# Gathered expert rows two units ahead, one pool for the weight rows, split dot products and another order of the gathers

## The chip, the core and the metric

The kernel runs on one core of a Trainium2 chip. The time is the device time of one execution in microseconds (us), the median of three runs. The core has five engines that run their own instruction lists in order and wait for each other by semaphores: TensorE (PE: matmuls; PEld is its weight load), VectorE (DVE), ScalarE (ACT), GpSimd (POOL) and SyncE (SP), which here only issues transfers. Indirect transfers (gathers) are issued on POOL. 16 DMA engines move the data.

## The reference

One decoder layer over 512 tokens of width 2048: RWKV-7 time mixing beside Mamba-2, an output projection, then an expert layer (PEER). The change lies in the expert layer alone. For each token it picks, in 8 heads, 16 of 16384 experts:

```python
q = (xb @ w_query).reshape(PEER_BLOCK, PEER_HEADS, 2, PEER_HALF)
s = jnp.einsum('lhpd,hpnd->lhpn', q, sub_keys).astype(jnp.float32)
s_half, i_half = lax.top_k(s, PEER_TOPK)
...
top_s, pos = lax.top_k(cand_s, PEER_TOPK)
eidx = jnp.take_along_axis(cand_i, pos, axis=-1)
gates = jax.nn.softmax(top_s, axis=-1)
u = u_emb[eidx]
act = jax.nn.gelu(jnp.einsum('ld,lhkd->lhk', xb, u), approximate=False)
return jnp.einsum('lhk,lhkd->ld', gates * act, v_emb[eidx])
```

`u_emb` and `v_emb` are 16384 x 2048 float32 tables, 134 MB each. A residual add and a final RMSNorm follow.

## The kernel before

The first 1640 us (projections, scan, output projection, queries and top-k) are the same code before and after, but for the pool that the query weights pass through. Then the 512 tokens are treated in two ways.

**320 tokens (TD) go dense, through all experts.** `expert_u(i)` multiplies 128 experts' u with the tokens: four quarter rows of 256 KB are loaded (`load_split`), each is split into a high part (a ScalarE cast, line 193) and a low part (a POOL subtraction, line 194), and TensorE does 3 matmuls for each of 16 blocks, 48 in all (lines 197 to 199). 128 such calls cover u. `expert_v(grp)` does the same with v for 512 experts in four quarters; a quarter again has four splits (`vhi`, `vlo`) and 48 matmuls, into `po`, which VectorE adds to `hT` (line 1197). One `expert_u` or one quarter of `expert_v` is called a unit; there are 256. Between the two, `gate_block` builds the gate matrix with two VectorE operations per token (J and I2, lines 1115 and 1116) and a matmul, by way of DRAM (`glD`); `expert_g` multiplies gates and activations on VectorE (line 1155) and splits them (`glo`). The first 30 `expert_u` stand ahead of the first `expert_v`; their activations go through DRAM.

**192 tokens (TG) are gathered.** Each slot gathers 128 rows of 8 KB, 1 MB, by an indirect transfer that POOL issues (line 1225). A u slot is a row per token, and one VectorE instruction multiplies it with the token's row and sums it (the dot, line 1230). 128 tokens have 128 slots (`("u", 0, n)`); the other 64 lie twice on the partitions and have 64 (`("u", 1, n)`). A v slot is the 128 rows of one token, and TensorE sums them with weights: four slots are collected, then four parts (`part(q)`) of 16 small matmuls go out (line 1245, `pw`). A part is written to DRAM (`yG`); `gathered()` reads it back, adds and normalises.

**What sets the order.** `pace(ins)` is called after each unit. It uses the rows gathered at the last call, then issues at most two gathers, as long as fewer than NGB rows are held and the slots lie behind units / NGU. A part is taken from `parts` after each split in `expert_v`. The instruction order on each engine is then made by a scheduler from this trace of calls. Rows for u and v have their own pools: `wr` 3 quarter rows with 3 pairs of high and low parts (pool `wp`), `vr` 3 half rows (512 KB) with 3 pairs (pool `vp`).

Of the kernel before, what the change touches and what calls it, by code (L numbers as in the profile page):

```python
# [10 lines left out]
F32 = mybir.dt.float32  # L11
# [8 lines left out]
P = 128  # L20
T = 512
# [5 lines left out]
TD = 320  # L27
NGU = 236
TG = T - TD
TB = 32  # L30
NGB = 6
NACT = 9
NSP = 30
# [96 lines left out]
def _hybrid(st, tc, nc, I, out):  # L130
# [56 lines left out]

    copied = []
    done_mm = [None]

# [43 lines left out]
    with ExitStack() as sb:  # L234
# [97 lines left out]

        wp = sc.enter_context(tc.tile_pool(name="wp", bufs=3, reuse_waits="tile"))
        bp = sb.enter_context(tc.tile_pool(name="bp", bufs=1, reuse_waits="tile"))
        lora = bp.tile([P, 3, T], F32, name="lora")
# [6 lines left out]
        def load_split(w, q, n):  # L342

            wr = wp.tile([P, n, P], F32, name="wr", bufs=3)
            nc.sync.dma_start(wr, w[:, q:q + n, :])
            whi = wp.tile([P, n, P], F32R, name="whi")
            wlo = wp.tile([P, n, P], F32R, name="wlo")
            return whi, wlo, split(whi, wlo, wr, G)

        def project_to(pss, ws, xhi, xlo, ahead=()):  # L350

            nk = ws.shape[2]
            ahead = list(ahead)
            for q in range(0, nk, 4):
                n = min(4, nk - q)
                for j, ps in enumerate(pss):
                    whi, wlo, last = ahead.pop(0) if ahead else load_split(ws[j], q, n)
                    for i in range(n):
                        k = q + i
                        mm3(ps, whi[:, i, :], wlo[:, i, :], xhi[k], xlo[k], k == 0, k == nk - 1)  # L360
            return last

# [573 lines left out]


    pu = st.enter_context(tc.tile_pool(name="pu", bufs=2, space=PSUM, reuse_waits="tile"))
    pw2 = st.enter_context(tc.tile_pool(name="pw2", bufs=1, space=PSUM, reuse_waits="tile"))
# [4 lines left out]
    gt_st = ExitStack()  # L944
    va = st.enter_context(tc.tile_pool(name="va", bufs=NACT, reuse_waits="tile"))
    gq = st.enter_context(tc.tile_pool(name="gq", bufs=1, reuse_waits="tile"))
# [4 lines left out]

    n2t = gq.tile([P, D], F32, name="row")
    n2D = dp.tile([P, D], F32, name="n2D")
    yG = dp.tile([TG, D], F32, name="yG")
# [4 lines left out]
    with ExitStack() as s3:  # L959
# [17 lines left out]
        for k in range(KT):  # L977
            t = qp.tile([P, T], F32, name="t")
            for h, c in ((hT[k], slice(0, TD)), (hG[k], slice(TD, T))):
                V.scalar_tensor_tensor(t[:, c], h, w2[:, k:k + 1], rr[:, c], OP.mult, OP.mult)  # L980
            nc.sync.dma_start(hGD[:, k, :], hG[k])
            nf = qp.tile([P, T], F32, name="nf")
            if k % 2:
                V.tensor_scalar_add(nf, t, mod2[:, 16 + k:17 + k])
            else:
                S.activation(nf, t, AF.Identity, bias=mod2[:, 16 + k:17 + k])
            split(nhi[k], nlo[k], nf[:, 0:TD], V if k % 4 == 0 else G)
            split(ngh[k], ngl[k], nf[:, TD:T], V if k % 4 == 2 else G)
            if k % 4 == 0:
                pt = [pq.tile([P, 4, P], F32, name="sc") for _ in range(2)]  # L990
            TE.transpose(pt[0][:, k % 4, :], nf[:, T - P:T], ident)
            TE.transpose(pt[1][0:64, k % 4, :], nf[:, TD:TD + 64], ident)
            if k % 4 == 3:
                S.copy(n2t[:, P * (k - 3):P * (k + 1)], pt[0].rearrange("p a b -> p (a b)"))
                n2s = qp.tile([64, T], F32, name="n2s")
                S.copy(n2s, pt[1][0:64].rearrange("p a b -> p (a b)"))
                for half in range(2):
                    nc.sync.dma_start(n2D[64 * half:64 * half + 64, P * (k - 3):P * (k + 1)], n2s)
        skT = qp.tile([P, 16, P], F32, name="skT", bufs=1)
# [98 lines left out]

    hg_st.close()
    gr = st.enter_context(tc.tile_pool(name="gr", bufs=NGB, side="right", reuse_waits="tile"))  # L1100
    gx = gt_st.enter_context(tc.tile_pool(name="gx", bufs=2, reuse_waits="tile"))
# [4 lines left out]
    def gate_block(tb):  # L1106

        gb = gx.tile([P, P, TB], F32, name="gb", bufs=1)
        for q in range(TB // 4):
            ps = pg.tile([P, 4, P], F32, name="pg")  # L1110
            for i in range(4):
                t = TB * tb + 4 * q + i
                J = gx.tile([P, P], F32, name="J", bufs=12)
                I2 = gx.tile([P, P], F32, name="I2", bufs=12)
                V.tensor_scalar(J, iota, jT[:, t:t + 1], None, OP.is_equal)  # L1115
                V.tensor_scalar(I2, iota, iT[:, t:t + 1], gT[:, t:t + 1], OP.is_equal, OP.mult)  # L1116
                TE.matmul(ps[:, i], lhsT=J, rhs=I2, start=True, stop=True)
# [16 lines left out]

    slots = [("u", 0, n) for n in range(P)]
    for n in range(P):
        slots += [("u", 1, n // 2)] * (n % 2 == 0) + [("v", 64 + n)]
    slots += [("v", n) for n in range(64)]
    nslots = len(slots)
# [22 lines left out]
    def pace(ins):  # L1162

        nonlocal units
        units += 1
        with tc.issue_after(ins.ins):
            ready, begun[:] = begun[:], []
            for s in ready:
                use(*s)
            while slots and (nslots - len(slots)) * NGU < units * nslots and len(begun) < 2 and held[0] < NGB:  # L1170
                begun.append(gather(slots.pop(0)))

    vrows = I["v"].rearrange("(g i j) c -> g j i c", i=4, j=P)

    def expert_v(grp):
        nonlocal nu
        gh = ghl.pop(grp)
        for q in range(4):
            po = [pv.tile([P, TD], F32, name="po") for _ in range(4)]
            for i in range(4):  # L1180
                if i % 2 == 0:
                    vr = vp.tile([P, 2, 512], F32, name="vr", bufs=3)
                    nc.sync.dma_start(vr, vrows[grp][:, i:i + 2, 512 * q:512 * q + 512])
                vhi = vp.tile([P, 512], F32R, name="vhi", bufs=3)
                vlo = vp.tile([P, 512], F32R, name="vlo", bufs=3)
                last = split(vhi, vlo, vr[:, i % 2, :], G)
                for d in range(4):
# [16 lines left out]
            if not (slots or begun or parts or done):  # L1204
                done.append(True)
                gathered()
            if nu < min(128, 4 * grp + 12):
                pace(expert_u(nu))
                nu += 1

    wts = [gq.tile([P, n], F32, name=f"wts{n}") for n in (P, 64)]
    begun = []
    parts = []
    four = []
    held = [0]
    n2s = [n2t]

    def gather(s):
        g = gr.tile([P, D], F32, name="g")
        if s[0] == "u" and s[1] and s[2] == 0:  # L1220
            n2s.append(gq.tile([P, D], F32, name="row"))
            nc.sync.dma_start(n2s[1], n2D)
        held[0] += 1
# [4 lines left out]
    def use(g, kind, i, n=None):  # L1228
        if kind == "u":
            V.scalar_tensor_tensor(g, g, 1.0, n2s[i], OP.mult, OP.mult, accum_out=wts[i][:, n:n + 1])  # L1230
            held[0] -= 1
# [23 lines left out]
    def weights(i):  # L1255

        w = wts[i]
        S.activation(w, w, AF.Gelu)
        V.tensor_tensor(w, w, ggt[i], OP.mult)
# [50 lines left out]
    for grp in range(32):  # L1310
        expert_g(grp)
        expert_v(grp)


    rr = rms_all(pu, "mm", gq, sacc[:, 0:TD])
# [29 lines left out]
```

## Time and profile before

| | |
|---|---|
| median of 3 runs | 4291.24 us (4290.52 to 4294.44) |
| the profiled execution | 4301.42 us |
| its span, first to last instruction | 4299.7 us |
| busy: PE / DVE / ACT / POOL | 90% / 56% / 33% / 58% of the span |
| mean granted TensorE clock | 0.930 of full speed |
| moved | 956.51 MB, mean 222 GB/s |
| dots on VectorE (line 1230) | 192, mean 3095 ns |
| subtractions on POOL, u and query / v | 832, mean 1366 ns / 512, mean 1420 ns |

A busy PE is not a PE at its peak: each dense matmul's record is 0.31 us long, while the next starts about 0.15 us after it. So TensorE's pace is read from starts, not from its busy share. The granted clock is 1.0 at 2.4 GHz and 0.5 at 1.2 GHz; values between are mixtures. Idle time of an engine that nobody waits for costs nothing.

### The profile page before, as it was taken

The page shows a single profiled execution, that of the slowest core. Times are in us where ns is not written, and L with a number is a line of the kernel's source. Part 1 is how long each engine was busy: PE and PEld are TensorE (multiplying, and loading weights), DVE is VectorE, ACT ScalarE, POOL GpSimd, SP SyncE. Part 2 cuts the span into 40 slices and gives each one's busy share as a digit, 9 for nine tenths or more (in the row PEclk, how much of TensorE's full clock was granted, in tenths as well). Part 3 has the DMA queues.
Part 4 walks back from the last instruction along what each step waited for, and adds up shares of the span by engine and source line. Part 5 has one row for each costly group of instructions (what it writes and reads, how often), then busy time and mean ns, then how long its engine had stood idle before and what let it go on. Part 6 is the DMA issues. An engine that isn't in the chain of part 4 may idle for free.

```text
span 4299.7 us, 64989 instructions
## 1 busy us (share of the span) xinstructions
PE 3870.1 (90%) x23694; PEld 3119.5 (73%) x23694; DVE 2414.9 (56%) x4523; ACT 1427.3 (33%) x2780; POOL 2507.4 (58%) x1919
## 2 busy tenths in 40 slices
PE   5899989999998997877788779999999999999976
PEld 3667657766667996776777768888787788777736
DVE  7442254556516999992778874445555545422204
ACT  3443233333324222332222223333333333333313
POOL 5455434423236334455777888777777778766633
PEclk9999989978979998888899889999999999999977
DMA  8456642242433226667877878888788888877762
GB/s 341 169 186 208 193 122 77 77 122 78 154 106 106 72 83 243 234 243 247 295 261 273 317 264 294 302 310 295 282 298 302 303 307 309 295 265 256 275 236 97
DMA packets 373681, 956.51 MB, mean 222 GB/s; under 512 B 57904, under 2 KB 123312, under 8 KB 317872
## 3 DMA queue, kind: packets, MB, share of 16 engines
q1 hardware_dynamic: 318064, 549.68, 38.7%
q0 software_dynamic: 55296, 402.68, 24.6%
q8 instruction: 186, 3.05, 0.3%
q14 instruction: 135, 1.11, 0.1%
HBM read 907.92 MB, written 44.24 MB: 221 GB/s over the span
## 4 chain that ended last, share of the span: by engine, by line
PE 63%; DVE 17%; DMA 8%; POOL 5%; issue 3%; ACT 1%; SPq 0%; POOLq 0%; DVEq 0%; ACTq 0%
PE mm L199 9%; PE mm L197 9%; PE mm L198 9%; PE pw L1245 7%; PE po L197 6%; PE po L199 6%; PE po L198 6%; DVE I L1116 3%; DVE g L1230 2%; DMA wr<-in_uT 2%; DVE J L1115 2%; POOL vlo L194 2%; POOL wlo L194 1%; DMA AI<-abD 1%; POOL g L1225 1%
## 5 line engine op out<-in xcount | busy, mean ns | idle before, releaser
L194 POOL TENSOR_TENSOR wlo<-wr,whi 128x512 fp32r<-128x512 f32 (+2 forms) x832 | 1127.6, 1366 | 965.9 <-ACT whi L193 866.5
L194 POOL TENSOR_TENSOR vlo<-vr,vhi 128x512 fp32r<-128x512 f32 x512 | 719.3, 1420 | 244.9 <-ACT vhi L193 211.6
L197 PE MATMUL mm<-n2hi,whi 128*128 128x320 f32 x2304 | 756.8, 329 | 53.7 <-ACT whi L193 52.9
L199 PE MATMUL mm<-n2hi,wlo 128*128 128x320 f32 x2304 | 751.9, 328 | 52.8 <-POOL wlo L194 52.6
L193 ACT CAST whi<-wr 128x512 fp32r<-128x512 f32 (+2 forms) x832 | 503.3, 616 | 861.9 <-PE mm L198 429.2
L198 PE MATMUL mm<-n2lo,whi 128*128 128x320 f32 x2304 | 741.6, 322 | 0.0
L197 PE MATMUL po<-ghi,vhi 128*128 128x320 f32 x2048 | 646.5, 322 | 50.6 <-DVE hT L1197 43.5
L1230 DVE SCALAR_TENSOR_TENSOR g<-g,row 128x2048 f32<-128x2048 f32 x192 | 591.6, 3095 | 168.7 <-DMA g<-in_u,eix 168.7
L198 PE MATMUL po<-glo,vhi 128*128 128x320 f32 x2048 | 640.4, 316 | 0.5 <-DVE glo L194 0.5
L199 PE MATMUL po<-ghi,vlo 128*128 128x320 f32 x2048 | 565.5, 320 | 51.2 <-POOL vlo L194 51.0
L193 ACT CAST vhi<-vr 128x512 fp32r<-128x512 f32 x512 | 312.9, 619 | 706.6 <-PE po L198 557.8
L199 PEld LDWEIGHTS mm<-n2hi,wlo 128*128 128x128 f32 x2304 | 456.6, 199 | 102.7 <-POOL wlo L194 68.2
L197 PEld LDWEIGHTS mm<-n2hi,whi 128*128 128x128 f32 x2304 | 458.0, 199 | 90.5 <-ACT whi L193 64.2
L197 PEld LDWEIGHTS po<-ghi,vhi 128*128 128x128 f32 x2048 | 394.9, 194 | 131.8 <-issue 57.9
L1197 DVE SCALAR_TENSOR_TENSOR hT<-po,mod,hT 128x320 f32<-128x320 f32 x512 | 250.8, 542 | 389.4 <-PE po L199 389.4
L198 PEld LDWEIGHTS mm<-n2lo,whi 128*128 128x128 f32 x2304 | 457.7, 199 | 14.1 <-issue 13.4
L199 PEld LDWEIGHTS po<-ghi,vlo 128*128 128x128 f32 x2048 | 370.4, 193 | 117.6 <-POOL vlo L194 68.8
L1155 DVE TENSOR_TENSOR act<-gd,act 128x320 f32<-128x320 f32 x128 | 214.1, 1687 | 422.4 <-ACT act L1128 392.2
L198 PEld LDWEIGHTS po<-glo,vhi 128*128 128x128 f32 x2048 | 396.3, 193 | 27.7 <-issue 26.8
L1245 PE MATMUL pw<-g,wT 128*32 128x512 f32 x1536 | 327.2, 631 | 31.2 <-DMA g<-in_v,eT 21.3
L1225 POOL DMA_INDIRECT g<-in_u,eix x192 | 247.8, 1291 | 93.7 <-PE pw L1245 23.8
L1225 POOL DMA_INDIRECT g<-in_v,eT x192 | 184.7, 962 | 160.9 <-DVE g L1230 75.5
(438 smaller groups left out, 5899.7 us busy)
## 6 DMA issues: line engine op xcount, KB each, us to landing
wr<-in_uT SPq DMA_DIRECT2D x512, 256.0 KB
vr<-in_v SPq DMA_DIRECT2D x256, 512.0 KB
wr<-in_wrest SPq DMA_DIRECT2D x160, 256.0 KB
aw<-in_ada SPq DMA_DIRECT2D x32, 1024.0 KB
a2w<-in_adar SPq DMA_DIRECT2D x64, 512.0 KB
glD<-gb SPq DMA_DIRECT2D x10, 2048.0 KB
gd<-glD SPq DMA_DIRECT2D x32, 640.0 KB
a3w<-in_adar SPq DMA_DIRECT2D x32, 512.0 KB
```

The costliest lines, as they stand in the source:

```text
L193: copied.append(S.copy(hi, src))
L194: return (eng or V).tensor_tensor(lo, src, hi.bitcast(F32), OP.subtract)
L197: TE.matmul(ps, lhsT=whi, rhs=xhi, start=first, stop=False)
L198: TE.matmul(ps, lhsT=whi, rhs=xlo, start=False, stop=False)
L199: done_mm[0] = TE.matmul(ps, lhsT=wlo, rhs=xhi, start=False, stop=last)
L1115: V.tensor_scalar(J, iota, jT[:, t:t + 1], None, OP.is_equal)
L1116: V.tensor_scalar(I2, iota, iT[:, t:t + 1], gT[:, t:t + 1], OP.is_equal, OP.mult)
L1155: V.tensor_tensor(a.rearrange("p (b t) -> p b t", t=TB), gd[:, :, i, :], a.rearrange("p (b t) -> p b t", t=TB), OP.mult)
L1197: V.scalar_tensor_tensor(h, po[d], mod2[:, 48 + k:49 + k], h, OP.mult, OP.add)
L1225: G.indirect_dma_start(out=g, out_offset=None, in_=I[s[0]], in_offset=bass.IndirectOffsetOnAxis(ap=ix, axis=0))
L1230: V.scalar_tensor_tensor(g, g, 1.0, n2s[i], OP.mult, OP.mult, accum_out=wts[i][:, n:n + 1])
L1245: TE.matmul(ps[32 * j:32 * j + 32, :], lhsT=wT[:, t0 + j:t0 + j + 1].to_broadcast([P, 32]), rhs=gs[j][:, cq], start=True, stop=True, tile_ ...
```

## The change

- **One pool.** When the output projection is done, pool `wp` is closed and another opened with ten quarter rows (`NRAW`) and four pairs of parts (`NSPL`); u and v rows share them. A v load is now a quarter row of 256 KB (512 loads instead of 256). J and I2 have 4 buffers instead of 12.
- **Gathers.** A gather's row is used two calls of `pace` later (`LEAD`). Seven rows instead of six, and the slots are laid over 200 units instead of 236. Parts are now also taken inside `project_to`, so in `expert_u` too. A loop at the end takes what is left.
- **Dots in halves.** A dot becomes two instructions of 1024 elements and one addition for all slots at the end.
- **Order of slots.** The 64 two-slot u gathers come first, then four v, then the 128 others with one v behind each second one, then the rest of v.
- The tokens' row (`row`) is loaded from DRAM for both groups, into one buffer. Activations have 6 buffers instead of 9, and `expert_u` runs at most 8 instead of 12 ahead.

```diff
-NGU = 236
+NGU = 200
-NGB = 6
-NACT = 9
+NGB = 7
+LEAD = 2
+NRAW = 10
+NSPL = 4
+NACT = 6
...
                         mm3(ps, whi[:, i, :], wlo[:, i, :], xhi[k], xlo[k], k == 0, k == nk - 1)
+                if parts:
+                    parts.pop(0)()
...
+    sc.close()
+    wp = st.enter_context(tc.tile_pool(name="wx", bufs=NSPL, reuse_waits="tile"))
+    nraw = NRAW
...
-                J = gx.tile([P, P], F32, name="J", bufs=12)
-                I2 = gx.tile([P, P], F32, name="I2", bufs=12)
+                J = gx.tile([P, P], F32, name="J", bufs=4)
+                I2 = gx.tile([P, P], F32, name="I2", bufs=4)
...
-    slots = [("u", 0, n) for n in range(P)]
+    slots = [("u", 1, n) for n in range(64)] + [("v", n) for n in range(4)]
     for n in range(P):
-        slots += [("u", 1, n // 2)] * (n % 2 == 0) + [("v", 64 + n)]
-    slots += [("v", n) for n in range(64)]
+        slots += [("u", 0, n)] + [("v", 4 + n // 2)] * (n % 2 and n < 120)
+    slots += [("v", n) for n in range(64, TG)]
...
-            ready, begun[:] = begun[:], []
-            for s in ready:
-                use(*s)
-            while slots and (nslots - len(slots)) * NGU < units * nslots and len(begun) < 2 and held[0] < NGB:
-                begun.append(gather(slots.pop(0)))
+            while begun and begun[0][0] <= units - LEAD:
+                use(*begun.pop(0)[1:])
+            for _ in range(2):
+                if slots and (nslots - len(slots)) * NGU < units * nslots and held[0] < NGB:
+                    begun.append((units,) + gather(slots.pop(0)))
...
-                if i % 2 == 0:
-                    vr = vp.tile([P, 2, 512], F32, name="vr", bufs=3)
-                    nc.sync.dma_start(vr, vrows[grp][:, i:i + 2, 512 * q:512 * q + 512])
-                vhi = vp.tile([P, 512], F32R, name="vhi", bufs=3)
-                vlo = vp.tile([P, 512], F32R, name="vlo", bufs=3)
-                last = split(vhi, vlo, vr[:, i % 2, :], G)
+                vr = wp.tile([P, 512], F32, name="vr", tag="wr", bufs=NRAW)
+                nc.sync.dma_start(vr, vrows[grp][:, i, 512 * q:512 * q + 512])
+                vhi = wp.tile([P, 512], F32R, name="vhi", tag="whi")
+                vlo = wp.tile([P, 512], F32R, name="vlo", tag="wlo")
+                last = split(vhi, vlo, vr, G)
...
-            if nu < min(128, 4 * grp + 12):
+            if nu < min(128, 4 * grp + 8):
...
-        if s[0] == "u" and s[1] and s[2] == 0:
-            n2s.append(gq.tile([P, D], F32, name="row"))
-            nc.sync.dma_start(n2s[1], n2D)
+        if s[0] == "u" and s[2] == 0:
+            n2s[s[1]] = va.tile([P, D], F32, name="row", bufs=1)
+            nc.sync.dma_start(n2s[s[1]], n2D[s[1]])
...
-            V.scalar_tensor_tensor(g, g, 1.0, n2s[i], OP.mult, OP.mult, accum_out=wts[i][:, n:n + 1])
+            for e in range(2):
+                c = slice(D // 2 * e, D // 2 * e + D // 2)
+                V.scalar_tensor_tensor(g[:, c], g[:, c], 1.0, n2s[i][:, c], OP.mult, OP.mult,
+                                       accum_out=wtp[i][:, e, n:n + 1])
...
+    while slots or begun or parts:
+        while parts:
+            parts.pop(0)()
+        pace(done_mm[0])
+    if not done:
+        gathered()
```

The instruction order of TensorE where the gates end (`pg` is a gate matmul, `mm` one of `expert_u`, `po` one of `expert_v`), before:

```order
L1117 MATMUL pg<-I_16623,J 128x128
L1117 MATMUL pg<-I_16628,J 128x128
L199 MATMUL mm<-n2hi_11444,wlo 128x320
L197 MATMUL mm<-n2hi_11445,whi 128x320
L198 MATMUL mm<-n2lo_11461,whi 128x320
```

and after:

```order
L1128 MATMUL pg<-I_16636,J 128x128
L1128 MATMUL pg<-I_16641,J 128x128
L201 MATMUL po<-ghi,vhi 128x320 x4
L202 MATMUL po<-glo,vhi 128x320
L203 MATMUL po<-ghi,vlo 128x320
```

Before, some ten units of `expert_u` follow the last gate; after, the last 50 gate matmuls stand together and `expert_v` follows at once.

POOL near unit 60, in the units of `expert_v` and `expert_u` that alternate (`g<-in_u` and `g<-in_v` are gathers), before:

```order
L1225 DMA g<-in_u,eix_11494 128x2048 x3
L194 TENSOR_TENSOR vlo<-vr,vhi 128x512 x3
L194 TENSOR_TENSOR wlo<-wr,whi 128x512 x2
L194 TENSOR_TENSOR vlo<-vr,vhi 128x512
L1225 DMA g<-in_u,eix_11494 128x2048 x3
```

and after:

```order
L198 TENSOR_TENSOR wlo<-wr,whi 128x512 x4
L198 TENSOR_TENSOR vlo<-vr,vhi 128x512
L1235 DMA g<-in_v,eT 128x2048
L1235 DMA g<-in_u,eix_11494 128x2048 x2
L1235 DMA g<-in_v,eT 128x2048
L198 TENSOR_TENSOR vlo<-vr,vhi 128x512
```

Gathers of v, which need no dot, have come between those of u.

TensorE at the last parts of the gathered tokens (`pw`; four matmuls are one part, and `mm<-ident,g` belongs to `gathered()`), before:

```order
L197 MATMUL po<-ghi,vhi 128x320
L198 MATMUL po<-glo,vhi 128x320
L1245 MATMUL pw<-g,wT 32x512 x4
L199 MATMUL po<-ghi,vlo 128x320 x4
L1245 MATMUL pw<-g,wT 32x512 x52
L1284 MATMUL mm<-ident,g 128x64
```

and after:

```order
L201 MATMUL po<-ghi,vhi 128x320
L202 MATMUL po<-glo,vhi 128x320
L203 MATMUL po<-ghi,vlo 128x320
L1258 MATMUL pw<-g,wT 32x512 x29
L1298 MATMUL mm<-ident,g 128x64
```

52 matmuls in a row have become 29. Behind them 384 dense matmuls (8 units) are left before, 1008 (21 units) after.

## Rows read from the trace of the kernel before

**Rows 1.** Line 194 by stretch: DVE (calls), POOL (calls), clock, DMA share, GB/s.

```profile
1640.00:2075.00 435.00, 1.69 (x4) 162.46 (x111) 0.86 0.71 255
2075.00:2600.00 525.00, 50.00 (x37) 296.45 (x202) 0.90 0.80 285
2600.00:3130.00 530.00, 43.47 (x28) 323.21 (x237) 0.99 0.83 296
3130.00:3750.00 620.00, 71.04 (x36) 370.90 (x272) 1.00 0.84 303
3750.00:4100.00 350.00, 26.32 (x19) 187.93 (x149) 1.00 0.74 268
4100.00:4300.00 200.00, 3.64 (x4) 49.22 (x39) 0.74 0.43 151
```

**Rows 2.** Timeline of PE from 3907: start, us, instruction.

```profile
3907.09 0.31 PE L198 MATMUL mm<-n2lo,whi 128*128 128x320 f32 x1
3907.32 1.06 PE L1245 MATMUL pw<-g,wT 128*32 128x512 f32 x8
3908.57 0.31 PE L197 MATMUL mm<-n2hi,whi 128*128 128x320 f32 x1
...
3911.80 0.31 PE L198 MATMUL mm<-n2lo,whi 128*128 128x320 f32 x1
```

**Rows 3.** Lines on DVE, 1640 to 1930: calls, busy us, mean ns, idle before.

```profile
L1116 DVE TENSOR_SCALAR I<-iota,iT,gT 128x128 f32<-128x128 f32 x314 | 145.0, 462 | 0.0
...
L1230 DVE SCALAR_TENSOR_TENSOR g<-g,row 128x2048 f32<-128x2048 f32 x33 | 80.7, 2475 | 0.0
```

**Rows 4.** Timeline of DVE and POOL from 2452.

```profile
2452.81 5.18 DVE L1230 SCALAR_TENSOR_TENSOR g<-g,row 128x2048 f32<-128x2048 f32 x1
...
2453.28 2.56 POOL L194 TENSOR_TENSOR vlo<-vr,vhi 128x512 fp32r<-128x512 f32 x2
...
2457.92 2.28 DVE L1230 SCALAR_TENSOR_TENSOR g<-g,row 128x2048 f32<-128x2048 f32 x1
2458.27 2.77 POOL L1225 DMA_INDIRECT g<-in_u,eix  x1 [2.44 <-DVE g L1230]
...
2460.14 2.28 DVE L1230 SCALAR_TENSOR_TENSOR g<-g,row 128x2048 f32<-128x2048 f32 x1
```

**Rows 5.** Lines, 2075 to 2600: dots and gather issues.

```profile
L1230 DVE SCALAR_TENSOR_TENSOR g<-g,row 128x2048 f32<-128x2048 f32 x79 | 263.2, 3351 | 19.7 <-DMA g<-in_u,eix 19.7
...
L1225 POOL DMA_INDIRECT g<-in_u,eix x79 | 123.1, 1558 | 26.8 <-issue 8.3 <-DVE g L1230 7.3 <-PE po L199 4.1
```

**Rows 6.** Line 1225, gathers: ns min/median/max, waits on POOL, landing.

```profile
L1225 POOL DMA_INDIRECT g<-in_v,eT x192: 933/940/1877, 2580.9 to 4170.0; - x192
...
  DVE g L1230: 89.4, 30
...
DMA to landing us min/median/max: 5.5/8.8/15.3
```

**Rows 7.** Chain of waits at the end: start, us, what.

```profile
4161.18 1.98 PE pw L1245 x8
...
4163.86 1.98 PE pw L1245 x8
...
4169.98 10.33 DMA g<-in_v,eT
...
4191.92 3.85 DMA yG<-ys
...
4217.03 1.00 PE mm L928 x4
...
4284.03 1.45 PE mm L928 x6
```

**Rows 8.** Waits from 1900 on: us in total, times, longest.

```profile
ACT whi L193 <- DMA wr<-in_uT: 152.4, 59, 8.0
```

**Rows 9.** Waits of PE, 3750 to 4100.

```profile
PE pw L1245 <- DMA g<-in_v,eT: 0.8, 1, 0.8
```

More of the change, by code (lines that the diff above doesn't have):

```diff
@@ L188, in _hybrid @@
     copied = []
+    parts = []
     done_mm = [None]
@@ L333, in _hybrid @@
         wp = sc.enter_context(tc.tile_pool(name="wp", bufs=3, reuse_waits="tile"))
+        nraw = 3
         bp = sb.enter_context(tc.tile_pool(name="bp", bufs=1, reuse_waits="tile"))
@@ L342, in load_split @@
         def load_split(w, q, n):
-            wr = wp.tile([P, n, P], F32, name="wr", bufs=3)
+            wr = wp.tile([P, n, P], F32, name="wr", bufs=nraw)
             nc.sync.dma_start(wr, w[:, q:q + n, :])
@@ L944, in _hybrid @@
     gt_st = ExitStack()
-    va = st.enter_context(tc.tile_pool(name="va", bufs=NACT, reuse_waits="tile"))
     gq = st.enter_context(tc.tile_pool(name="gq", bufs=1, reuse_waits="tile"))
@@ L950, in _hybrid @@
     gT = gp.tile([P, T], F32, name="gT")
-    n2t = gq.tile([P, D], F32, name="row")
-    n2D = dp.tile([P, D], F32, name="n2D")
+    n2D = dp.tile([2, P, D], F32, name="n2D")
     yG = dp.tile([TG, D], F32, name="yG")
@@ L993, in _hybrid @@
             if k % 4 == 3:
-                S.copy(n2t[:, P * (k - 3):P * (k + 1)], pt[0].rearrange("p a b -> p (a b)"))
-                n2s = qp.tile([64, T], F32, name="n2s")
-                S.copy(n2s, pt[1][0:64].rearrange("p a b -> p (a b)"))
+                n2s = qp.tile([P, T], F32, name="n2s")
+                S.copy(n2s, pt[0].rearrange("p a b -> p (a b)"))
+                nc.sync.dma_start(n2D[0][:, P * (k - 3):P * (k + 1)], n2s)
+                n2s = qp.tile([P, T], F32, name="n2s")
+                S.copy(n2s[0:64], pt[1][0:64].rearrange("p a b -> p (a b)"))
                 for half in range(2):
-                    nc.sync.dma_start(n2D[64 * half:64 * half + 64, P * (k - 3):P * (k + 1)], n2s)
+                    nc.sync.dma_start(n2D[1][64 * half:64 * half + 64, P * (k - 3):P * (k + 1)], n2s[0:64])
         skT = qp.tile([P, 16, P], F32, name="skT", bufs=1)
@@ L1099, in _hybrid @@
     hg_st.close()
+    va = st.enter_context(tc.tile_pool(name="va", bufs=NACT, side="right", reuse_waits="tile"))
     gr = st.enter_context(tc.tile_pool(name="gr", bufs=NGB, side="right", reuse_waits="tile"))
@@ L1211, in _hybrid @@
     wts = [gq.tile([P, n], F32, name=f"wts{n}") for n in (P, 64)]
+    wtp = [gq.tile([P, 2, n], F32, name=f"wtp{n}") for n in (P, 64)]
     begun = []
-    parts = []
     four = []
     held = [0]
-    n2s = [n2t]
+    n2s = {}
     def gather(s):
         g = gr.tile([P, D], F32, name="g")
-        if s[0] == "u" and s[1] and s[2] == 0:
-            n2s.append(gq.tile([P, D], F32, name="row"))
-            nc.sync.dma_start(n2s[1], n2D)
+        if s[0] == "u" and s[2] == 0:
+            n2s[s[1]] = va.tile([P, D], F32, name="row", bufs=1)
+            nc.sync.dma_start(n2s[s[1]], n2D[s[1]])
         held[0] += 1
@@ L1257, in weights @@
         w = wts[i]
+        V.tensor_tensor(w, wtp[i][:, 0], wtp[i][:, 1], OP.add)
         S.activation(w, w, AF.Gelu)
```

## The prediction

> **What bounds the kernel now.** I read the span in stretches first, then asked for each stretch which engine another one waits for. The unit of counting is a unit of dense work: one `expert_u` or one quarter of `expert_v`, each 4 splits and 48 matmuls, 256 in all. The split's subtraction on POOL (line 194) counts them: its calls by stretch, divided by 4, are units [rows 1]. About 3 units lie ahead of 1640 us; then 28 units take 435 us (15.5 each), 50.5 take 525 (10.4), 59 take 530 (8.95), 68 take 620 (9.1), 37 take 350 (9.4), and the last 10 take 200.
>
> TensorE's own price of a unit: dense matmuls start 0.147 us apart (22 starts from 3908.57 to 3911.80), so 48 are 7.04 us. Where one part of a gathered v (8 short matmul records) stands between them, two starts take 1.48 us (3907.09 to 3908.57) instead of 0.29, so a part costs 1.19 [rows 2]. There is one part per v row, 192 in all. From 3750 to 4100 two parts per unit give 7.04 + 2.38 = 9.4, which is what the stretch shows: TensorE is the bound there. Elsewhere it is not.
>
> In the 290 us up to 1930 VectorE has no idle time before its gate operations and dots [rows 3]. 33 dots at 2.28 leave 215 us for 314 gate pairs, 0.68 each. From 2075 to 2600 VectorE and POOL block each other. A dot that is 2.28 us alone lasts 5.18 when two subtractions (1.28 each) run inside it, and a gather issue that is 0.94 alone lasts 2.77 beside a dot [rows 4, 6]. A unit there has 4 subtractions (5.12), 1.56 dots (3.57) and 1.6 gather issues (1.5): 10.2 in sum, 10.4 measured [rows 1, 5]. So the sum of what POOL and VectorE do with SBUF operands is the price of a unit there, TensorE's 7 us notwithstanding, and the granted clock is 0.90. The last 200 us are a drain: the chain of waits alternates gathers of up to 10.3 us with v parts 2.68 us apart, at clock 0.74; then the gathered tokens' end runs from 4191.9 to 4217, and only then the last 8 units [rows 1, 7].
>
> **The change, part by part.** No computation goes; what moves is when things stand where. I counted gathers against units in the instruction order of both programs. Before: 49 gathers issued by unit 31, 219 by unit 141 (159 of them u), 384 by 256. After: 58, 235 (176 u), and 379 by unit 235.
>
> *Ahead of unit 31.* Gates now lie evenly between 30 units instead of 20, so V can't start before the last gate. VectorE needs 320 x 0.68 = 218 us of gates and 58 dots. A half dot was never run: at least 1.14 (half of 2.28), at most 1.14 plus a blocked subtraction, 2.4; I take 1.2, since a half saves nothing of its start, so 2.4 a dot, 139 us. Sum 357; J and I2 with four buffers instead of twelve and blocked dots make it 390 (my bounds 355 and 450), then some 25 us until the last gate block has gone through DRAM and V begins, in place of other units that used to cover it. That is 415 for what took 435: V begins near 2055 instead of 2075.
>
> *Units 31 to 141.* Dots go from 110 to 118 and gathers from 170 to 177, but before they crowd into the first 50 units. Evenly spread, a unit has 5.12 of subtractions, 1.07 dots at 2.4 (2.57) and 1.6 gather issues (1.5): 9.2, and TensorE's side is 7.04 plus half a part, 7.7. With the ratio of measured to summed (10.4 to 10.2) that is 9.4 a unit, 110 units in 1034 us instead of 1055. Bounds: 8.95, the price from 2600 to 3130 where a unit had half a dot, and 10.4, that of the crowded stretch.
>
> The loads' own part of this I cost at zero. ScalarE waited 152 us for u rows [rows 8], yet behind those waits stands the POOL sum, which does not shrink. Counted in the instruction order, ten shared quarter rows let a load go out 20 us and more of TensorE work ahead of its use (9 to 20 before). On the other hand four shared hi/lo pairs replace three and three; what queues behind a late split is the next gather, on POOL.
>
> *Units 141 to 235.* 94 units at 7.04 are 662; 128 v parts at 1.19 are 152; 2% for near ties, 16. Sum 830. Few dots are left here (16), so POOL's 5.12 + 1.5 stays below TensorE.
>
> *The end.* Before, 13 of the last v parts stand back to back behind all but 8 units. Now 7 do, with 21 units behind them. I charge 7 x 2.68 = 19, one gather wait of 10 and the same 25 for the gathered tokens: 54. Then 8 units at the 8.4 that the last 8 took (4217 to 4284 [rows 7]) and 13 at 7.04: 159. The close from 4284 on is unchanged, 16.
>
> Moved with these: the 128-token row is loaded from DRAM in one megabyte behind the 64th dot of the other group, on the sync queue ahead of later loads; at ten rows of stock that hides, and costs some 10 us if the stock is out. The 256 more load issues on that queue lie beside its waiting. The extra additions are two.
>
> **Sum**, against the profiled span of 4299.7: 2055 + 1034 + 830 + 54 + 159 + 16 = 4148, 152 less. The profiled execution took 4301.4 and the median is 4291.2; the same 152 off the median gives 4139, and I say 4140.
>
> **The rivals.**
> - *Loads and halves help more.* Waits of ScalarE on loads go, blocked POOL stretches halve, the crowded stretch reaches 8.7 a unit and the first one saves 40 more: 77 + 40 less, 4020. For it: those 152 us of waits. Against: no stretch with a dot has shown under 8.95.
> - *POOL and VectorE don't overlap at all.* The gather issue that began at 2458.27 waited out one dot and ended beside the next, which stayed at 2.28 us [rows 4], so some overlap exists. If a half dot locks POOL as a whole one did, and each hand-over costs a wait, a unit is 10.3: 110 x 0.9 = 99 more, 4240. The trace's 10.4 for a sum of 10.2 is close to no overlap already, which keeps it alive. The Trainium skill has this as a rule (SBUF — State Buffer, section "SBUF: two separate sides"): GpSimd and a VectorE operation with two SBUF inputs hold one port pair exclusively for the whole instruction. By that rule, halving a dot divides the longest block and leaves the sum; the 5.18 us dot agrees.
> - *The fourth gather of a token group is late.* After unit 141 a group's rows come free together, and the next group's last gather has 8 to 10 us of TensorE work to land, against 8.8 median [rows 6]. At 2.5 us for each of 32 groups: 80 more, 4220. Against it: the same distance held from 3750 to 4100, and TensorE's waits for gathers there are 0.8 us in sum [rows 9].
> - *Slower: gathers stand at POOL's head.* Seven rows with a lead of two units leave a gather waiting for the dot just queued. Each such wait was 3.0 us before (89.4 in 30) [rows 6], with the splits of the next unit behind it. If every unit from 31 to 141 pays one of them in half a unit's reach, 1.5 us, that is 165 more: 4305. It decides from 10.8 us a unit on. Against it: the lead also means that the dot no longer waits for its data (in the instruction order a v gather stands 3 units of TensorE work ahead of its use, 2.4 before).
>
> **Chances.** Forecast 0.52 (its own range 4095 to 4190), better 0.15, no overlap 0.12, late fourth gather 0.11, slower 0.10. This kernel's timing tells 0.2%, 8.6 us. From the slower case 0.07 lies above that and 0.03 within it; with some of the overlap case, faster 0.87, same 0.05, slower 0.08. Eight in ten: 4035, where the better case begins to be left out, to 4265.
>
> **What would show it.** Units by the subtraction's calls: 9.4 us from unit 31 to 141, 8.8 from there to 235, TensorE at clock 1.0; v parts before the last 160 us with no alternation of gathers and parts but one; VectorE's gates ending near 2030; ScalarE's waits for loads near zero. Wrong if a unit in the middle costs over 10, or POOL's waits for dots exceed 150 us.

## The result and the profile after

The changed kernel takes 4177.5 us (median of four runs, 4163.62 to 4187.0) where the kernel before takes 4292.56: a ratio of 0.9729, 95% interval 0.9699 to 0.976. Forecast was 4140, range 4035 to 4265. The profiled execution has a span of 4180.8 us, 119 less than before; forecast were 152 less. In the four stages of the sum:

| stage | forecast us | changed | before |
|---|---|---|---|
| first matmul of V starts at | 2055 | 2054.5 | 2065 |
| from there to unit 141 | 1034 | 1020 | 1062 |
| units 141 to 235 | 830 | 874 | 860 |
| unit 235 to the end | 229 | 232 | 313 |

So three terms came out within 15 us and one, the third, 44 too low. The stages can be read from POOL's subtractions. Line 198 of the changed kernel by stretch (columns: VectorE's calls, POOL's calls, granted clock, share of the DMA engines, GB/s), which answers to [rows 1]:

```profile
1640.00:2055.00 415.00, 0.00 (x0) 157.08 (x108) 0.87 0.76 278
2055.00:3075.00 1020.00, 120.65 (x71) 613.91 (x440) 0.98 0.86 309
3075.00:3949.00 874.00, 54.34 (x46) 490.60 (x377) 1.00 0.82 299
3949.00:4181.00 232.00, 8.75 (x11) 108.59 (x84) 0.85 0.44 146
```

The same line (194) of the kernel before in the stretches that hold the same units:

```profile
2065.00:3127.00 1062.00, 95.16 (x69) 622.45 (x439) 0.94 0.82 290
3127.00:3987.00 860.00, 87.07 (x48) 503.15 (x376) 1.00 0.81 292
3987.00:4300.00 313.00, 13.93 (x11) 107.28 (x85) 0.83 0.55 197
```

POOL's calls divided by four are units: 110 (440 calls), 94 (377) and 21 (84). A unit now costs 9.3 us in the middle, 9.3 in the third stretch.

VectorE's lines from 1640 to 2040 (calls, busy us, mean ns, idle before) answer to [rows 3]:

```profile
L1127 DVE TENSOR_SCALAR I<-iota,iT,gT 128x128 f32<-128x128 f32 x309 | 160.1, 518 | 0.0
L1242 DVE SCALAR_TENSOR_TENSOR g<-g,row 128x1024 f32<-128x1024 f32 x118 | 153.8, 1337 | 0.0
L1126 DVE TENSOR_SCALAR J<-iota,jT 128x128 f32<-128x128 f32 x309 | 137.9, 446 | 3.8 <-PE pg L1128 3.7
```

VectorE has again next to no idle time until the gates are done, now with 118 half dots (59 dots, 1.30 us of busy time each half) among them. The first matmul of V in the changed kernel, then in the kernel before:

```profile
2054.53 1.44 PE L201 MATMUL po<-ghi,vhi 128*128 128x320 f32 x4 [13.10 <-ACT ghi L197]
```

```profile
2065.09 1.17 PE L197 MATMUL po<-ghi,vhi 128*128 128x320 f32 x3 [2.62 <-ACT ghi L193]
```

In the third stretch TensorE sets the pace. Its timeline there (start, us, instruction), which answers to [rows 2]:

```profile
3502.52 0.31 PE L203 MATMUL po<-ghi,vlo 128*128 128x320 f32 x1
3502.76 1.06 PE L1258 MATMUL pw<-g,wT 128*32 128x512 f32 x8
3503.76 0.41 PE L201 MATMUL po<-ghi,vhi 128*128 128x320 f32 x1
...
3516.65 0.31 PE L203 MATMUL po<-ghi,vlo 128*128 128x320 f32 x1
3516.89 1.06 PE L1258 MATMUL pw<-g,wT 128*32 128x512 f32 x6
3517.88 0.41 PE L201 MATMUL po<-ghi,vhi 128*128 128x320 f32 x1
...
3521.36 0.31 PE L202 MATMUL po<-glo,vhi 128*128 128x320 f32 x1
3521.60 1.04 PE L1258 MATMUL pw<-g,wT 128*32 128x512 f32 x2
3522.57 0.41 PE L201 MATMUL po<-ghi,vhi 128*128 128x320 f32 x1
```

The first stop is a whole part, four rows in 8 records. The other two are one part torn in two: three rows (6 records), and the fourth row 4.7 us later (2 records). From dense start to dense start they take 1.24, 1.23 and 1.21 us instead of 0.15, and the start after that comes 0.25 us later instead of 0.15: 1.17 to 1.19 in sum. A stop has a price, a row has next to none.

The end, on TensorE (with what ended an idle time, in brackets), answers to [rows 7]:

```profile
3956.18 1.04 PE L1258 MATMUL pw<-g,wT 128*32 128x512 f32 x2
...
3975.53 1.91 PE L1258 MATMUL pw<-g,wT 128*32 128x512 f32 x2 [4.77 <-DMA g<-in_v,eT]
3978.16 1.93 PE L1258 MATMUL pw<-g,wT 128*32 128x512 f32 x8 [0.72 <-ACT ys L1261]
...
3983.53 1.94 PE L1258 MATMUL pw<-g,wT 128*32 128x512 f32 x8 [0.75 <-ACT ys L1261]
3996.09 0.36 PE L1298 MATMUL mm<-ident,g 64*128 64x64 f32 x1 [10.62 <-DMA g<-yG]
```

One run of 7 parts is left, 2.68 us apart at its end, then the gathered tokens' transposes, and behind them dense work at 7.04 us a unit, its price at full pace.

### The profile page after: what moved, and what is told of

Its sections match the earlier page's. It is cut to its first block, busy times and chain, and to the rows that moved or that the text cites. A ratio compares the mean times of both kernels' runs of the same rounds, so it can differ in the third digit from the quotient of the medians.

```text
span 4180.8 us, 65986 instructions
## 1 busy us (share of the span) xinstructions
PE 3789.5 (91%) x23694; PEld 3071.0 (73%) x23694; DVE 2403.2 (57%) x4909; ACT 1433.6 (34%) x2778; POOL 2475.7 (59%) x1919
## 5 line engine op out<-in xcount | busy, mean ns | idle before, releaser
L198 POOL TENSOR_TENSOR vlo<-vr,vhi 128x512 fp32r<-128x512 f32 x512 | 695.1, 1375 | 236.8 <-ACT vhi L197 213.4
L201 PE MATMUL mm<-n2hi,whi 128*128 128x320 f32 x2304 | 735.3, 320 | 11.6 <-ACT whi L197 9.2
L201 PE MATMUL po<-ghi,vhi 128*128 128x320 f32 x2048 | 627.9, 316 | 38.9 <-DVE hT L1207 18.8
L1242 DVE SCALAR_TENSOR_TENSOR g<-g,row 128x1024 f32<-128x1024 f32 x384 | 616.5, 1645 | 5.4 <-DMA g<-in_u,eix 5.4
L203 PE MATMUL po<-ghi,vlo 128*128 128x320 f32 x2048 | 527.7, 318 | 25.2 <-POOL vlo L198 24.7
L203 PEld LDWEIGHTS mm<-n2hi,wlo 128*128 128x128 f32 x2304 | 440.3, 191 | 99.4 <-issue 48.6
L1166 DVE TENSOR_TENSOR act<-gd,act 128x320 f32<-128x320 f32 x128 | 162.5, 1279 | 605.2 <-ACT act L1139 528.0
L1258 PE MATMUL pw<-g,wT 128*32 128x512 f32 x1536 | 293.6, 617 | 20.2 <-ACT ys L1261 11.6
L1235 POOL DMA_INDIRECT g<-in_u,eix x192 | 227.7, 1186 | 120.5 <-DVE I L1127 29.2
L201 PE MATMUL mm<-nhi,whi 128*128 128x512 f32 x640 | 261.4, 408 | 4.5 <-ACT whi L197 4.5
```

The lines of the kernel that those rows point to most:

```text
L198: return (eng or V).tensor_tensor(lo, src, hi.bitcast(F32), OP.subtract)
L201: TE.matmul(ps, lhsT=whi, rhs=xhi, start=first, stop=False)
L203: done_mm[0] = TE.matmul(ps, lhsT=wlo, rhs=xhi, start=False, stop=last)
L1166: V.tensor_tensor(a.rearrange("p (b t) -> p b t", t=TB), gd[:, :, i, :], a.rearrange("p (b t) -> p b t", t=TB), OP.mult)
L1235: G.indirect_dma_start(out=g, out_offset=None, in_=I[s[0]], in_offset=bass.IndirectOffsetOnAxis(ap=ix, axis=0))
L1242: V.scalar_tensor_tensor(g[:, c], g[:, c], 1.0, n2s[i][:, c], OP.mult, OP.mult, accum_out=wtp[i][:, e, n:n + 1])
```

## Experiments

The units are counted in every run as above, and a stop is a group of gathered-row matmuls with dense matmuls on both sides. "The middle" is the time from V's first matmul to unit 141, "the third stretch" that from unit 141 to 235. The middle does not hold the same work in every run: the scheduler puts 113 dots and 175 gathers there in the changed kernel, 108 and 170 before. Where a run differs by more than a few, it is said.

**1. The rows of a part together.**

```diff
-            for j in range(4):
-                TE.matmul(ps[32 * j:32 * j + 32, :], ...)
+            with tc.issue_after(row(3).ins):
+                for j in range(3):
+                    row(j)
```

> The changed kernel, with the four row matmuls of a v part kept together: the last row's is issued first, the other three behind it. In the instruction order TensorE then stops 123 times instead of 164 for gathered rows between units 141 and 235, and 59 times instead of 98 between 31 and 141; the burst at the end grows from 29 rows to 44 (about 4 parts more). Theory S (a stop costs 1.19 us, whether one row or four stand in it): units 141 to 235 take 874 - 41 x 1.19 = 825 us, the end costs 4 x 2.68 = 11 more, and 31 to 141, where POOL and VectorE set the pace, gains between 0 and 46; the whole 4095 to 4140. Rival R (what I missed between 141 and 235 are late fourth gathers): a part now waits for its last row as a whole, nothing is saved, 4180 to 4260.

Measured: 4187.7 us, ratio 0.9734 (0.9714 to 0.9753), no gain: theory S missed. Yet the stops did go. In the trace there are 124 instead of 163 between units 141 and 235, and that stretch takes 858 us instead of 874: 16 of 39 x 1.19 = 46 came. The middle stayed (1026 instead of 1020, though 41 stops went there too), and the end is 13 longer for its longer run. TensorE's waits in that stretch (us in all, times, longest) in the changed kernel:

```profile
PE po L203 <- POOL vlo L198: 6.1, 6, 3.2
PE mm L203 <- POOL wlo L198: 4.3, 6, 1.4
PE pw L1258 <- DMA g<-in_v,eT: 3.4, 6, 1.0
```

and with the rows together:

```profile
PE pw L1258 <- DMA g<-in_v,eT: 10.8, 13, 1.4
PE mm L203 <- POOL wlo L198: 9.7, 14, 2.7
PE pw L1280 <- DVE wts L1277: 5.9, 1, 5.9
PE po L203 <- POOL vlo L198: 5.5, 3, 3.0
```

About 20 us of what was saved stand there as waits. The granted clock of the stretch is lower too, 0.99 instead of 1.00:

```profile
3089.00:3947.00 858.00, 87.69 (x47) 487.00 (x377) 0.99 0.82 298
```

In the trace some 20 us of it are at 1.2 GHz; had TensorE been the bound all that time, they cost 10 (an estimate). So 16 saved, 20 of waits and up to 10 of clock account for the 46, as far as waits and clock don't overlap. The whole lies in rival R's range, but its cause does not hold: waits for gathers are 10.8 us, not 80.

**2. Dots whole again.** Line 1242's loop over two halves goes; the rest stays.

> The changed kernel with each dot product in one instruction of 2048 columns instead of two of 1024; all else the same. Theory (the sum of POOL's and VectorE's work is the price, halving only divides the block): units 31 to 141 within 15 us of 1022, the whole 4165 to 4195. Rival (the halves are what made that stretch faster, by letting gathers and splits in between): back to 10.4 us a unit there from 9.3, 110 x 1.1 = 120 more, about 4300.

Measured: 4231.2, ratio 0.9829 (0.9801 to 0.9857), 54 us above the changed kernel by the medians, 43 by the two ratios. Theory and rival both missed, it lies between them: V begins 13 later (2068), the middle takes 1051 (31 more), the third stretch 888 (14 more), the end is 10 shorter. So halving is worth between a third and a half of the gain of 115, more than I gave it. The middle's row (busy us of PE, PEld, DVE, ACT and POOL, then clock, DMA share, GB/s):

```profile
2068.00:3119.00 1051.00, 952.40 (x5778) 825.16 (x5779) 674.64 (x646) 335.98 (x615) 865.02 (x618) 0.96 0.85 302
```

VectorE and POOL are busy for 1540 us here, and for 1541 in the changed kernel's middle (its row stands at run 5): halving left that sum alone (time that one of them was blocked is in it), and the time fell all the same.

**3. The pace of before in the changed kernel** (`NGU = 236`).

> The changed kernel with the gathers paced over 236 units as before instead of 200. In the instruction order the last part stands at unit 253.6, with 33 stops from unit 235 on and a run of only 2 parts at the end. Theory 1 (the end was long before because 13 parts stood back to back; that came from rows and lead, not from the pace): the cost is only the gathered tokens' end (25 plus a gather wait of 10) without dense work beside it, less up to 20 in the middle, where a unit has 0.9 dots instead of 1.07: 4185 to 4215. Rival (the pace alone removed the drain): the whole 80 us of the end come back, 4255 or more.

Measured: 4169.4, ratio 0.9693 (0.9674 to 0.9712), which can't be told from the changed kernel's. From unit 235 to the end it takes 250 us instead of 232, the third stretch 854 instead of 874, and V begins 12 earlier (2043). The drain does not come back: the rival fell. Theory 1's range was missed too, by 16 us: the end costs 18 more and not 35.

**4. The kernel before with the rows together** (the edit of 1).

> The kernel before, with nothing changed but the row matmuls of a part kept together as in the first of these runs. Stops between units 141 and 235: 108 instead of 159, from 235 on 11 instead of 21, a burst of 64 rows instead of 52 (3 parts more). Theory S: 51 x 1.19 = 61 and 10 x 1.19 = 12 less, 8 more at the end: 4227, 4205 to 4245. Rival R (late gathers): 4280 to 4330.

Measured: 4291.6, ratio 0.9981 (0.9965 to 0.9997). Again the stops go (154 to 105 between units 141 and 235) and little time: 15 of 49 x 1.19 = 58 us in that stretch, while the end grows by 10. TensorE's waits in the stretch are 42 us instead of 16, most of them for VectorE's additions to `hT` and ScalarE's casts, and the granted clock is 0.97 instead of 1.00, some 50 us at 1.2 GHz and by the same estimate up to 25 of time. The larger of these waits, and the stretch:

```profile
PE po L197 <- DVE hT L1197: 17.3, 7, 6.6
PE po L197 <- ACT vhi L193: 16.1, 3, 6.0
```

```profile
3128.00:3973.00 845.00, 68.52 (x48) 502.47 (x377) 0.97 0.82 293
```

Theory S missed here too. The time lies in rival R's range, but TensorE waits 1.4 us for gathers there. Whether the clock falls because of the waits, or for another reason, is not shown.

**5 and 6. Less and more of the dots.**

```diff
-            for e in range(2):
+            for e in range(2 if units <= NSP else 1):              # 5
+            for e in ((0, 1) if units <= NSP else (0, 1, 0, 1)):   # 6
```

> The changed kernel with the second half of each dot product left out for the slots used after unit 30 (the sums then hold half the columns); the gathers, their rows and all else stay. In the middle (from V's begin to unit 141, 1021 us) a half dot took 1.74 us on average. Theory (the sum of POOL's and VectorE's work is the price there): 118 x 1.15 to 1.74 = 136 to 200 less, down to TensorE's own 7.04 plus a stop a unit, so 890 to 920, and the whole 4045 to 4080. Rival (VectorE is off the path there; POOL with ScalarE's casts, or the 306 GB/s of transfers, set the pace): the middle within 35 us of 1021, the whole 4140 to 4185.

> The changed kernel with each half dot done twice for the slots used after unit 30 (the row is multiplied in a second time). Theory (sum of POOL and VectorE): the middle grows by 118 x 2.3 to 3.5 us, 270 to 410, the whole 4440 to 4590. Rival (VectorE is 70% busy there and has some 300 us of idle time that takes the second half dots): up to 60 more, 4180 to 4240.

Measured: 4127.6 (ratio 0.9611, 0.958 to 0.9642) and 4420.1 (1.0292, 1.0258 to 1.0326). The middle takes 1003 us with half the dot work and 1175 with twice. The middle of run 5 and of run 6 (columns as in run 2):

```profile
2054.00:3057.00 1003.00, 941.64 (x5812) 815.16 (x5812) 515.36 (x656) 339.62 (x618) 793.24 (x627) 0.98 0.89 323
```

```profile
2065.00:3240.00 1175.00, 996.57 (x5766) 858.32 (x5766) 1072.66 (x1290) 337.91 (x612) 923.51 (x608) 0.92 0.75 262
```

The changed kernel's own row is this:

```profile
2055.00:3075.00 1020.00, 939.07 (x5758) 812.06 (x5758) 720.12 (x866) 332.45 (x610) 820.83 (x615) 0.98 0.86 309
```

VectorE loses 205 us of busy time in run 5 and the stretch 17, the whole 50: there the sum of POOL and VectorE is not what sets the pace. The 17 are not quite clean, as this middle holds 120 dots and 187 gathers. In run 6 VectorE gains 353 and the stretch 155, with VectorE busy 91% of it: more dots do bind. The theory missed in both runs. The rival held for the middle of run 5 (within 35) and missed its whole by 12; in run 6 it missed. So the present load seems to lie at the edge between the two.

**7. The pace of the changed kernel in the kernel before** (`NGU = 200`).

> The kernel before with its gathers paced over 200 units instead of 236 and nothing else. In the instruction order a run of 61 rows (15 parts) now stands at unit 229.8, where 52 (13 parts) stood at 243.2. A part in such a run cost 5.2 to 5.8 us in the four profiles so far. Theory (the long run at the end comes from six buffers and a lead of one unit, not from the pace): the run costs 10 more, and more dots and gathers crowd into units 31 to 141: 4275 to 4325. Rival (an earlier end of the gathers alone removes the drain): 60 to 80 less, 4215 to 4235.

Measured: 4309.2, ratio 1.0032 (1.0017 to 1.0046). The pace alone makes it 0.3% slower, as the theory had it; the rival fell.

**8. A lead of one unit** (`LEAD = 1`).

> The changed kernel with gathered rows used one unit after their gather instead of two, and nothing else. In the instruction order 58 parts then stand in one run at unit 200.6, and 63 stops fewer before it. Theory (the lead of two units is what keeps the parts between dense work; a part in a run costs 5.5 us, a stop 1.19): 58 x 5.5 = 319 for the run instead of 40, less 63 x 1.19 = 75: 204 more, 4380 (4320 to 4430). Rival (the run is hidden by what stands around it, or the seven buffers carry the gain): 4160 to 4220.

Measured: 4336.8, inside the theory's range, ratio 1.0103 (1.0082 to 1.0124), 159 us above the changed kernel. One run of 58 parts takes 253 us from its first record, at 3653, to the gathered tokens' transposes (4.4 each, where the theory had 5.5). The 300 us that hold it (columns as in run 2), and line 1258's waits in them, of matmuls and weight loads both:

```profile
3600.00:3900.00 300.00, 188.51 (x806) 55.14 (x798) 13.43 (x18) 55.51 (x96) 87.44 (x85) 0.60 0.66 249
```

```profile
  ACT ys L1261: 212.0, 114
  DMA g<-in_v,eT: 123.0, 30
```

TensorE waits for the copy of each part's result, then for the next rows, and its granted clock is 0.60 in these 300 us. This one number is worth more than the whole change: with it undone, the rest is slower than before.

**9. Half the bytes of the u gathers,** with half dots.

> The run with half dots, and besides each u gather after unit 30 fetches 1024 columns instead of 2048 (0.5 MB instead of 1; of another half row of u, so the sums mean nothing). Of the 301 MB that move between units 31 and 141, 62 go. Theory D (transfers, at 306 to 325 GB/s in that stretch, are the floor that the half dots ran into): the middle falls from 1003 us towards TensorE's own 7.04 x 110 + 106 x 1.19 = 900, to 900 to 950; the whole 4030 to 4075. Rival P (the ring of ScalarE's casts, POOL's subtractions and TensorE over four hi/lo pairs is the floor): the middle within 20 us of 1003, the whole 4100 to 4140.

Measured: 4077.5, ratio 0.947 (0.9443 to 0.9497). The middle takes 962 us, 41 less than in run 5 and 62 above TensorE's own 900. Its row (columns as in run 2):

```profile
2053.00:3015.00 962.00, 928.75 (x5830) 809.73 (x5831) 592.22 (x682) 346.61 (x622) 822.05 (x642) 0.98 0.85 285
```

Rival P fell. Theory D's ranges were missed by 12 and by 2.5 us: fewer bytes help, at 285 GB/s instead of 323, but not down to TensorE's price. And this middle holds more than that of run 5: 132 half dots instead of 120, which last 2.27 us on average instead of 1.75, and 202 gathers instead of 187. That, and not slower work alone, is VectorE's 77 us more of busy time. VectorE also waits 198.6 us for gathered rows, against 13.0 in run 5; the cause stays open.

**10 and 11. Five hi/lo pairs and eight rows;** in 11 also the rows together and a pace of 220.

```diff
-NRAW = 10
-NSPL = 4
+NRAW = 8
+NSPL = 5
```

> The changed kernel with five hi/lo pairs instead of four and eight rows in stock instead of ten. In the instruction order TensorE stops 134 times instead of 164 between units 141 and 235, 104 instead of 98 before, and no run of parts is left at the end (4 rows instead of 29 in the last). Both theories: the end takes 30 us less. Theory P (ring of four pairs): the middle falls from 1021 to 960 to 1000, the whole 4085 to 4130. Theory D (transfers): the middle within 15 of 1021, the whole 4125 to 4155. Rival (fewer rows in stock make loads late): 4180 or more.

> The changed kernel with five hi/lo pairs, eight rows in stock, the row matmuls of a part together, and the gathers paced over 220 units: in the instruction order 190 stops, 121 of them between units 141 and 235, 12 after, no long run. V's begin 2055 + 1021 + 855 (as in the first run) + 21 x 7.04 + 12 x 1.19 = 162 + 25 for the gathered tokens + 22: 4140, and 30 to 60 less if the ring of pairs was the floor of the middle: 4080 to 4150.

Measured: 4180.8, ratio 0.9716 (0.9693 to 0.974), and 4155.0, ratio 0.9646 (0.9619 to 0.9673). Line 198 by stretch, first of run 10, then of run 11:

```profile
2045.00:3146.00 1101.00, 88.13 (x72) 619.81 (x439) 0.96 0.87 313
3146.00:3969.00 823.00, 57.70 (x45) 478.34 (x376) 1.00 0.80 288
```

```profile
2049.00:3116.00 1067.00, 81.59 (x72) 628.20 (x439) 0.95 0.87 309
3116.00:3932.00 816.00, 56.80 (x45) 483.39 (x377) 1.00 0.84 297
```

The third stretch has 134 and 117 stops and takes 823 and 816: 94 x 7.04 + 134 x 1.19 = 821, and 801 with 117. Here fewer stops go with less time; but of the changed kernel's 19 dots in this stretch none is left in run 10 and 12 in run 11. The middle went the wrong way, to 1101 and 1067. It holds 132 and 125 dots instead of 113, and 203 and 190 gathers instead of 175, and with eight rows ScalarE waits there 63 and 48 us for loads instead of 6. Theory P missed its ranges, but what a fifth pair is worth by itself the two runs don't tell. In run 10 the rival's range (4180 or more) holds; run 11 lies 5 us above its own. Run 11 is the fastest kernel of the study that computes everything, 0.8% below the changed one, with intervals apart.

**12. Six rows in the pool** (`NRAW = 6`).

> The changed kernel with six rows in the pool of quarter rows instead of ten. In the instruction order a load then goes out less far ahead, the last gate stands at unit 23.6 instead of 27.6, and the last run has 8 rows instead of 29. Theory (the stock of rows is worth nothing, as I forecast): the middle within 15 us of 1021, the whole 4140 to 4190. Rival (the stock carries part of the gain): ScalarE waits for loads, the middle 40 us longer or more, 4210 or more.

Measured: 4207.0, ratio 0.9777 (0.9753 to 0.9801), 29 us above the changed kernel by the medians, 21 by the ratios. The middle takes 1092 us, 72 more; an earlier V (13), the third stretch (17) and a shorter end (22) give most of it back. The theory fell; the rival held for the middle and missed its whole by 3. ScalarE's waits for loads in the middle, run 12 first, then the changed kernel:

```profile
ACT whi L197 <- DMA wr<-in_uT: 69.8, 33, 6.1
ACT vhi L197 <- DMA vr<-in_v: 55.7, 21, 8.2
```

```profile
ACT vhi L197 <- DMA wr<-in_uT: 4.2, 2, 2.2
ACT vhi L197 <- DMA vr<-in_v: 1.9, 2, 1.1
```

Not all of the 72 are late loads, for here too the middle holds more: 134 dots and 203 gathers instead of 113 and 175. The half dots of run 12's middle, then of the changed kernel's (count, busy us, mean ns, idle before):

```profile
L1242 DVE SCALAR_TENSOR_TENSOR g<-g,row 128x1024 f32<-128x1024 f32 x268 | 497.5, 1896 | 64.0 <-DMA g<-in_u,eix 64.0
```

```profile
L1242 DVE SCALAR_TENSOR_TENSOR g<-g,row 128x1024 f32<-128x1024 f32 x226 | 390.2, 1768 | 5.4 <-DMA g<-in_u,eix 5.4
```

By unit 235 both kernels have done all their dots, and run 12 is 42 us later there (3991 instead of 3949). In runs 10, 11 and 12 the middle is 81, 47 and 72 us longer with 19, 12 and 21 more dots, 3.4 to 4.3 us for each dot with the gathers that came along. What part of that is late loads and what part the moved work is not shown.

## Why the prediction was right, and where not

**Ahead of V: right.** Gates and dots fill VectorE until 2040 (forecast near 2030), V's first matmul follows 14 us later instead of 25, and V starts at 2054.5. Only the figure for before was off: its first V matmul starts at 2065, not 2075, so this stage gave 10 us and not 20.

**Units 31 to 141: the number right, two steps wrong, and in part luck.** I priced a unit at the sum of what POOL and VectorE do, and the loads at zero because "behind those waits stands the POOL sum". Run 5 refutes the first as a bound (205 us of VectorE's work for 17 of time), and so does run 2, where the same sum goes with 31 us more. Run 12 speaks against the second: with fewer rows in stock ScalarE waits 126 us for loads in this stage instead of 6, and the whole takes 21 to 29 us more. The 152.4 us of such waits before [rows 8] are counted from 1900 on; in this stage they were 42.0 for u and 31.9 for v, and they are near zero with ten rows, as forecast. How much of the 42 us gained in this stage is theirs I can't say: the kernel before had nine quarters in two pools, not six, and eight rows were only run together with a fifth pair. Halving alone accounts for 31 (run 2), which I had put at nothing beyond the even spread; all the rest of the change, loads and even spread together, is left with 11, as far as such parts add up. So 1034 came out near 1020 because the even spread, which I paid with 21, gave less and the halves gave more: two errors that cancelled. The granted clock of the stage rose from 0.94 to 0.98 along with it; whether that is a cause or only a sign of fewer waits no run here settles, but run 12 has 0.97 and takes 1092 us.

The Trainium skill's rule for the shared ports (SBUF — State Buffer, section "SBUF: two separate sides") says that of a VectorE operation with two SBUF inputs and a GpSimd operation that reads SBUF the second is shut out for the whole instruction of the first. The runs agree as to blocks: half dots of 1.22 us last 1.77 on average in the middle, and one lasts 7.67. That halving leaves the sum alone is what I took from it, and run 2 bears that out (1540 and 1541 us). What it does not bear out is the step from there to the time: 43 to 54 us come from halving alone.

**Units 141 to 235: the step that failed is "128 v parts at 1.19 are 152".** The 1.19 was right, but it belongs to a stop, not to a part. The scheduler issues a part's rows as they land, so 128 parts were 163 stops: 35 x 1.19 = 42 of the 44 us missed. It could have been seen: of 3750 to 4100 I read "two parts per unit", and that stretch has 50 parts in 37 units but 74 stops. The sum by stops is 662 + 163 x 1.19 = 856, and 18 of waits make 874. Runs 10 and 11 come out by that count within 2 and 15 us; the other kernels, without run 8 and its long run of parts, lie 8 to 59 above it, and most so runs 1, 4 and 6. Taking stops away is therefore not worth 1.19 each: in runs 1 and 4 only a quarter to a third of the saving came, and waits (for POOL, gathers and weights in run 1, for VectorE's additions and ScalarE's casts in run 4) and a lower granted clock stand in place of the rest. The two per cent for near ties (16) was about right. "Elsewhere it is not", said of TensorE as the bound ahead of 3750, was too narrow: before, 662 + 154 x 1.19 = 845 of the 860 us from 3127 to 3987 are its dense matmuls and stops.

**The end: right in sum,** 232 for 229, but by two errors that cancel: 66 us pass until the dense work behind the gathered tokens starts, at 4014.6 (54 forecast), and its 21 units take 149 (159 forecast). The 8.4 us read for each of the last 8 units before had the close of the gathered tokens ahead of them in it; from first to last their matmuls took 61 us, 7.6 each. What keeps the drain away in the changed kernel is the lead of two units: run 8 undoes it and gets a run of 58 parts. The pace did not do it (runs 3 and 7). The lead alone in the kernel before was not run, and neither were the seventh row, the order of the slots and the parts inside `expert_u` by themselves.

**The rivals.** "Loads and halves help more" was half right: halves help (run 2) and the stock of loads has a worth (run 12), but the middle did not reach 8.7 us. "No overlap" fell: a unit cost 9.3 us, not 10.3. "Late fourth gather" fell: TensorE waits 3.4 us for gathers in that stretch. "Slower" fell: POOL's waits for dots, line 1235 in the whole run, went from 89.4 [rows 6] to 36.3:

```profile
  DVE g L1242: 36.3, 17
```

## What to carry to other kernels

Count short matmuls that stand between others by the stops in the instruction order, not by the work in them; a scheduler that issues as data lands makes more stops than the code suggests. But don't expect the price of a stop back for each one removed: other waits may be next in line. A price that fits one stretch ("the sum of two engines") is shown only when work is taken away and time follows; where TensorE, POOL and the transfers are 80 to 92% busy, taking 205 us of work from VectorE gave 17, and adding 353 cost 155. A wait that looks covered can still be worth its cover: test the stock of loads by shrinking it. And before a stage's time is compared between two runs, count what work stands in it: in runs 10, 11 and 12 a setting moved 12 to 21 more dots into the stage that was looked at.

## What was not expected of the hardware

A stop of TensorE for one row (2 records) took 1.17 us beyond its dense matmuls and one for four rows (8 records) 1.19, medians of the changed kernel's trace between units 141 and 235. The matmuls of the four rows go to four groups of 32 output rows, and four records each start within 0.02 us: in this trace they run at once, 8 records in 1.06 us where 2 take 1.04.

A VectorE instruction that is short alone can last very long beside POOL: a subtraction of 128x320 with two SBUF inputs (0.48 us at its shortest) lasted 6.88, with five of POOL's subtractions in its time, one behind the other. Its record starts 0.32 us ahead of the first of the five and ends 0.35 us behind the last. VectorE, then POOL in the changed kernel, from 2496 (start, us, instruction):

```profile
2496.42 6.88 DVE L198 TENSOR_TENSOR glo<-act,ghi 128x320 fp32r<-128x320 f32 x1 [0.53 <-ACT ghi L197]
```

```profile
2496.74 2.54 POOL L198 TENSOR_TENSOR vlo<-vr,vhi 128x512 fp32r<-128x512 f32 x2
2499.25 3.70 POOL L198 TENSOR_TENSOR wlo<-wr,whi 128x512 fp32r<-128x512 f32 x3
```
